# The adaLN modulation computed a channel chunk at a time on TensorE, ahead of the first four blocks' projections

## The chip, the cores and the metric

One core of one Trainium2 chip runs the whole layer in one launch. The metric is the device time of that launch in microseconds (us). The profile names the engines PE (TensorE; PEld is its weight load), DVE (VectorE), ACT (ScalarE), POOL (GpSimd) and SP (SyncE, which here only issues DMAs).

## The reference, cut to what matters

```python
mod = jax.nn.silu(c) @ w_ada + b_ada                 # c (1,1024), w_ada (1024,3072)
shift, scale, gate = jnp.split(mod, 3, axis=-1)
h = rms_norm(x, norm_w) * (1.0 + scale) + shift      # x (2048,1024)
z = h @ w_in                                         # w_in (1024,10240)
a, b, g_conv, q, k, v, g_attn, m_conv, m_attn = jnp.split(z, SPLIT_POINTS, axis=-1)
q = rope(rms_norm(q, q_norm_w), positions)           # 12 heads of 128; k likewise
k = rope(rms_norm(k, k_norm_w), positions)
...  # dilated window attention, convolution branch, gates, two output projections
return x + gate * out
```

The change concerns what comes ahead of the first product with `w_in`: `mod` for shift and scale, the normalized and modulated `h` of the first tokens, and the sines and cosines of `rope`.

## The kernel before, in words

Tokens are cut into 16 blocks of 128 (`NB`), channels into 8 chunks of 128 (`KC`). `h` is kept transposed in SBUF for the whole kernel, as a rounded part `hi` and the rest `lo`; every weight chunk likewise as `wh` and `wl`. A projection of one block sums 24 matmuls, three (`wh·hi`, `wl·hi`, `wh·lo`) for each channel chunk.

The kernel goes through 12 attention units (one head each; q, k and v, 384 columns), then the gates, the convolution branch and the output. Unit 0 is special: while it is projected, `h` is still being made. The steps of that stage are:

- `load_x(j)` loads 128 tokens and returns four steps: two ACT squares (L199) whose sums go to POOL (an addition, L202, then `rsqrt_cols`, L106 and L107), and two ACT scalings (L207). They are "normalizing x of block j". Six `x` tiles exist.
- `h_turn`/`h_part(j, kk)` turn two blocks and two channel chunks with PE transposes (L217), apply scale and shift on DVE (L238), round on ACT (L241) and subtract on DVE (L242). `h_first` does that for blocks 0 and 1 from four groups of transposes made early.
- `load_w` loads a chunk of weights (`raw`, three tiles), copies it on ACT (L281, `wh`) and subtracts (L284, `wl`; for unit 0 on POOL).
- `project_step(u, j)` runs the 24 matmuls (`z_tokens`, L305) with hooks between them, then "the rope" of the block: ACT squares and copies v (L322, L329), POOL raises to −1/2, DVE makes q and k and rotates them (L333 to L343), and SP stores the result (L656). In unit 0, block j's hooks at the 12th and 20th matmul turn blocks two ahead; hooks normalize x of block j + 4, loaded two blocks before.

Ahead of all this, modulation: `w_ada`'s first 2048 columns come as 16 DMAs of 512 KB (rows of 4 KB, ten tiles), and 64 matmuls with the one column `sc` as the stationary operand and 512 columns moving (L163) give rows of `mod`; ACT copies them, 16 small transposes make columns of them (L171), and DVE adds the bias. The rotary tables (`tab`) are made for all 16 blocks at once by 16 DVE operations of 1024 columns and two ACT sines.

The order on PE is the program's own (`manual_schedule`). On the other engines a scheduler chooses the order by its own estimates of times, except for instructions given to `keep_in_program_order`, which keep their order among each other. Each engine and SP's queue then run strictly in that order. A DMA also waits for the one that used its semaphore before it; eight are used in turn, so at most eight DMAs are under way.

Of the kernel before, what the change touches and what calls it, by code (L numbers as in the profile page):

```python
# [18 lines left out]
P = 128  # L19
# [35 lines left out]
def tile_hybrid_block(  # L55
# [55 lines left out]

    tab = tabs.tile([P, NB, 2, 64], F32, tag="tab", name="tab0")
    with pool("start", side="right") as st:
        nat = st.tile([4 * KC, P], F32, name="nat")
        cols = st.tile([P, 4 * KC], F32, name="cols")
        nc.sync.dma_start(nat[:KC, :], c.rearrange("b (k p) -> (b k) p", p=P))
        nc.sync.dma_start(nat[KC : 3 * KC, :], b_ada[: 2 * D].rearrange("(k p) -> k p", p=P))
        nc.sync.dma_start(nat[3 * KC :, :], norm_w.rearrange("(k p) -> k p", p=P))
        nc.sync.dma_start(wqk[:, 0, :], q_norm_w[None, :].to_broadcast([P, P]))
        nc.sync.dma_start(wqk[:, 1, :], k_norm_w[None, :].to_broadcast([P, P]))  # L120
        pos_i = st.tile([P, NB], I32, name="pos_i")
        nc.sync.dma_start(pos_i, positions.rearrange("b (j p) -> p (b j)", p=P))
        freq = st.tile([P, 64], F32, name="freq")
        nc.sync.dma_start(freq, inv_freq[None, :].to_broadcast([P, 64]))

        pt = bank("t", "pt_c")
        nc.tensor.transpose(pt[:, : 4 * KC], nat, ident[: 4 * KC, : 4 * KC])
        nc.vector.tensor_copy(cols, pt[:, : 4 * KC])
        th = st.tile([P, KC], F32, name="th_c")
        nc.scalar.activation(th, cols[:, :KC], AF.Tanh, scale=0.5)  # L130
        nc.vector.scalar_tensor_tensor(sc, th, 1.0, cols[:, :KC], op0=ALU.add, op1=ALU.mult)
        nc.vector.tensor_scalar(sc, sc, 0.5, None, op0=ALU.mult)

        pos_f = st.tile([P, NB], F32, name="pos_f")
        nc.vector.tensor_copy(pos_f, pos_i)
        a = tab[:, :, 0, :]
        n = tab[:, :, 1, :]
        nc.vector.tensor_tensor(a, pos_f[:, :, None].to_broadcast([P, NB, 64]),
                                freq[:, None, :].to_broadcast([P, NB, 64]), op=ALU.mult)

        na = st.tile([P, NB, 64], F32, name="na")
        nc.vector.tensor_scalar(n, a, 1.0 / (2 * math.pi), MAGIC, op0=ALU.mult, op1=ALU.add)
        nc.vector.tensor_scalar(n, n, -MAGIC, None, op0=ALU.add)
        nc.vector.tensor_scalar(na, n, MAGIC * 2048, None, op0=ALU.add)
        nc.vector.tensor_scalar(na, na, -MAGIC * 2048, None, op0=ALU.add)
        nc.vector.tensor_sub(n, n, na)
        for part in TWO_PI:
            for t in (na, n):
                nc.vector.scalar_tensor_tensor(a, t, -part, a, op0=ALU.mult, op1=ALU.add)
        nc.vector.tensor_scalar(a, a, -PI_LO, PI_LO, op0=ALU.max, op1=ALU.min)  # L150
        nc.scalar.activation(n, a, AF.Sin)
        nc.scalar.activation(a, a, AF.Sin, scale=0.5)
        tc.keep_in_program_order(nc.scalar.activation(th[:, :1], th[:, :1], AF.Exp))
        nc.vector.tensor_tensor(a, a, a, op=ALU.mult)
        nc.vector.tensor_scalar(a, a, -2.0, 1.0, op0=ALU.mult, op1=ALU.add)

        acc = [bank("z", "ada0"), bank("z", "ada1"), bank("s", "ada2"), bank("s", "ada3")]
        for k in range(KC):
            for half in range(2):
                wa = st.tile([P, D], F32, tag="wa", name=f"wada{k}_{half}", bufs=10)  # L160
                last_ada = nc.sync.dma_start(wa, w_ada[P * k : P * k + P, D * half : D * half + D])
                for i in range(2):
                    nc.tensor.matmul(acc[2 * half + i][:1, :], sc[:, k : k + 1], wa[:, 512 * i : 512 * i + 512],  # L163
                                     start=(k == 0), stop=(k == KC - 1))
        row = st.tile([1, 2 * D], F32, name="row")

        for i in range(4):
            nc.scalar.activation(row[:, 512 * i : 512 * i + 512], acc[i][:1, :], AF.Copy)
        pa = bank("z", "pt_ada")
        for k in range(2 * KC):  # L170
            nc.tensor.transpose(pa[:, k : k + 1], row[:, P * k : P * k + P], ident[:1, :1])  # L171
        nc.vector.tensor_add(mod, pa[:, : 2 * KC], cols[:, KC : 3 * KC])
        nc.vector.scalar_tensor_tensor(mod[:, KC:], mod[:, KC:], 1.0, cols[:, 3 * KC :], op0=ALU.add, op1=ALU.mult)

# [9 lines left out]
    xp = xpool_c.__enter__()  # L184
    hx = {}

    def load_x(j):

        xt = xp.tile([P, D], F32, tag="x", name=f"x{j}")
        i0 = nc.sync.dma_start(xt, x2[P * j : P * j + P, :])  # L190
        if j >= 4:
            tc.keep_in_program_order(i0)
# [51 lines left out]
    with tc.high_priority():  # L244
        for j in range(4):
            for f in load_x(j):
                f()
        turned = [h_turn(0, kk, "ttoo"[kk]) for kk in range(4)]


    spare = {}
# [865 lines left out]
```

## Time and profile before

| | us |
|---|---|
| three runs | 2533.59, 2529.49, 2529.74 |
| median | 2529.74 |
| the profiled execution | 2532.06 |
| its span (first to last instruction) | 2530.3 |
| PE busy in the span | 2495.4 |
| DVE, ACT, POOL busy | 1663.2, 756.8, 250.1 |

The profiled execution lies 2.3 us above the median of the runs; 1.8 us of it lie outside the span. PE is busy for 99% of the span, so what the kernel loses is found in the few places where PE is not. A "busy" PE can still be slow: matmuls are pipelined, and the clock that it is granted changes.

### The profile page before, as it was taken

To read this page: it belongs to the slowest core of one execution; us is meant where nothing else is said; L and a number is where in the kernel's file an instruction comes from. 1 tells how busy PE (TensorE), PEld (TensorE's weight loads), DVE (VectorE), ACT (ScalarE), POOL (GpSimd) and SP (SyncE) were. 2 spreads that over 40 slices of the span, in tenths; PEclk is the share of its full clock that TensorE was granted. 3 is DMA by queue.
4 is the path that set the end of the run, shared out by engine and by line. 5 is a ranking of instruction groups with operands and counts; after the bars stand their busy time and mean duration, and the time that the engine had idled before them with its cause. 6 is when DMAs were issued, how large, how long until landed. Compare 5 with 4: busy or idle time off the path is not lost.

```text
span 2530.3 us, 38239 instructions
## 1 busy us (share of the span) xinstructions
PE 2495.4 (99%) x13377; PEld 2222.5 (88%) x13377; DVE 1663.2 (66%) x3522; ACT 756.8 (30%) x2366; POOL 250.1 (10%) x503
## 2 busy tenths in 40 slices
PE   7999999999999999999999999999999999999999
PEld 3989999999999999999888888888888878888887
DVE  5855655555555555566799999879697718774333
ACT  5733343344334434444111111111111114331010
POOL 3421111111111111122000000000000000000000
PEclk9999999999999999999999999999999999999999
DMA  6333533344321111144112122121212249867343
GB/s 228 116 106 113 160 111 97 100 118 122 108 75 55 56 36 40 52 130 149 41 47 70 64 80 83 39 70 60 63 65 68 99 147 328 296 211 230 124 134 111
DMA packets 262653, 278.51 MB, mean 110 GB/s; under 512 B 25464, under 2 KB 195736, under 8 KB 262462
## 3 DMA queue, kind: packets, MB, share of 16 engines
q1 hardware_dynamic: 262462, 276.07, 34.3%
q8 instruction: 106, 1.74, 0.3%
q14 instruction: 85, 0.70, 0.1%
HBM read 175.12 MB, written 100.86 MB: 109 GB/s over the span
## 4 chain that ended last, share of the span: by engine, by line
PE 95%; DMA 2%; ACT 1%; DVE 1%; POOL 1%; issue 0%; SPq 0%; POOLq 0%; DVEq 0%; ACTq 0%
PE pz L305 30%; PE pg L755 20%; PE yc L897 7%; PE out L897 7%; PE pb L755 7%; PE pa L755 7%; PE ya L897 3%; PE pzg L305 3%; PE ps L377 3%; PE po L396 3%; PE ptq L367 2%; PE ptp L388 1%; PE ada L163 1%; DMA fraw<-in_w_attn_out_dram 1%; DMA raw_u<-in_w_in_dram 0%
## 5 line engine op out<-in xcount | busy, mean ns | idle before, releaser
L784 DVE SCALAR_TENSOR_TENSOR ca<-up,chan,ca 128x1024 f32<-128x1024 f32 x480 | 593.2, 1280 | 3.7
L305 PE MATMUL pz<-wh_u,hT_lo 128*128 128x384 f32 x1536 | 536.2, 349 | 1.3 <-POOL hT_lo L230 0.7
L305 PE MATMUL pz<-wh_u,hT_hi 128*128 128x384 f32 x1536 | 516.9, 337 | 5.3 <-ACT wh_u L281 2.6
L305 PE MATMUL pz<-wl_u,hT_hi 128*128 128x384 f32 x1536 | 517.7, 337 | 0.6 <-DVE wl_u L284 0.4
L333 DVE SCALAR_TENSOR_TENSOR qk<-pz,st,wqk 128x128 f32<-128x128 f32 x384 | 116.9, 346 | 332.2 <-POOL st L107 332.1
L755 PE MATMUL pg<-hT_hi,wh_gm 128*128 128x512 f32 x768 | 298.7, 389 | 0.3 <-DVE gt L815 0.3
L755 PE MATMUL pg<-hT_lo,wh_gm 128*128 128x512 f32 x768 | 298.6, 389 | 0.0
L755 PE MATMUL pg<-hT_hi,wl_gm 128*128 128x512 f32 x768 | 297.9, 389 | 0.0
L305 PEld LDWEIGHTS pz<-wh_u,hT_hi 128*128 128x128 f32 x1536 | 289.7, 189 | 8.7 <-ACT wh_u L281 3.5
L305 PEld LDWEIGHTS pz<-wh_u,hT_lo 128*128 128x128 f32 x1536 | 289.2, 188 | 3.5 <-POOL hT_lo L230 1.3
L305 PEld LDWEIGHTS pz<-wl_u,hT_hi 128*128 128x128 f32 x1536 | 288.8, 188 | 1.8 <-DVE wl_u L284 1.4
L369 ACT ACTIVATE qkT<-ptq 128x256 f32<-128x256 f32 x192 | 74.0, 385 | 419.2 <-PE ptq L367 418.6
L813 ACT ACTIVATE gt<-pg 128x512 f32<-128x512 f32 x96 | 57.1, 597 | 422.2 <-PE pg L755 422.2
L755 PEld LDWEIGHTS pg<-hT_hi,wh_gm 128*128 128x128 f32 x768 | 144.1, 188 | 30.7 <-DVE gt L815 0.7
L755 PEld LDWEIGHTS pg<-hT_hi,wl_gm 128*128 128x128 f32 x768 | 144.2, 188 | 30.0
L755 PEld LDWEIGHTS pg<-hT_lo,wh_gm 128*128 128x128 f32 x768 | 144.1, 188 | 29.7
L107 POOL TENSOR_TENSOR st<-st,mhalf 128x2 f32<-128x2 f32 x192 | 136.7, 712 | 16.0
L322 ACT ACTIVATE sq<-pz 128x128 bf16<-128x128 f32 x384 | 106.2, 277 | 93.2 <-PE pz L305 86.4
L106 POOL TENSOR_SCALAR st<-st 128x2 f32<-128x2 f32 x192 | 45.7, 238 | 811.8 <-ACT sq L322 811.8
L382 ACT ACTIVATE sm<-sm,osb 128x128 f32<-128x128 f32 (+1 forms) x192 | 88.8, 462 | 64.4 <-DVE osb L380 61.3
L755 PE MATMUL pb<-hT_hi,wh_ab 128*128 128x512 f32 x256 | 99.7, 389 | 0.0
L755 PE MATMUL pa<-hT_hi,wh_ab 128*128 128x512 f32 x256 | 99.6, 389 | 0.0
(332 smaller groups left out, 4639.0 us busy)
## 6 DMA issues: line engine op xcount, KB each, us to landing
qkv_d<-qkv SPq DMA_DIRECT2D x128, 192.0 KB, 2.2
raw_u<-in_w_in_dram SPq DMA_DIRECT2D x96, 192.0 KB, 3.1
lqk<-qkv_d SPq DMA_DIRECT2D x128, 128.0 KB, 2.2
acc_d<-osb SPq DMA_DIRECT2D x192, 65.0 KB, 1.6
at<-acc_d SPq DMA_DIRECT2D x64, 195.0 KB, 3.3
x<-in_x_dram SPq DMA_DIRECT2D x16, 512.0 KB
wada<-in_w_ada_dram SPq DMA_DIRECT2D x16, 512.0 KB, 7.1
lv<-qkv_d SPq DMA_DIRECT2D x128, 64.0 KB, 1.8
```

What stands on the lines that cost most here:

```text
L107: nc.gpsimd.tensor_tensor(dst, scratch[:, :n], mhalf[:, :n], op=ALU.pow)
L305: nc.tensor.matmul(pz[:, :width], a[:, k, P * j : P * j + P], w[:, :width], start=(m == 0), stop=(m == 23))
L322: nc.scalar.activation(sq, pz[:, P * i : P * i + P], AF.Square, scale=1.0 / math.sqrt(P), accum_out=st[:, i : i + 1])
L333: nc.vector.scalar_tensor_tensor(qk[:, 2 * i : 2 * i + 2].rearrange("p a b -> p (a b)"), pz[:, P * i : P * i + P], st[:, 2 + i : 3 + i], w ...
L369: nc.scalar.activation(qkT.rearrange("p a b -> p (a b)"), pt[:, :256], AF.Copy)
L377: nc.tensor.matmul(ps[:, P * i : P * i + P], box["q"][:, 0, :], kt[:, 1, :], start=True, stop=True)
L382: nc.scalar.activation(sm[:, :w], sm[:, :w], AF.Exp, scale=-1.0, bias=o[:, P : P + 1], accum_out=o[:, P + 1 : P + 2])
L396: nc.tensor.matmul(po[:, :P], box["pT"][:, P * i : P * i + P], vt, start=(i == 0), stop=(i == nk - 1))
L755: nc.tensor.matmul(pz, w[k][:, P * col : P * col + P], a[:, k, 512 * t : 512 * t + 512], start=(m == 0), stop=(m == 23))
L784: nc.vector.scalar_tensor_tensor(accs[c], up[:, t0 + i : t0 + i + 1024], chan[:, cb, i : i + 1], accs[c], op0=ALU.mult, op1=ALU.add)
L813: nc.scalar.activation(th, pz, AF.Tanh, scale=0.5)
L897: nc.tensor.matmul(pz, w, xx, start=(m == 0), stop=(m == len(terms) - 1))
```

## The change

The function for the first four blocks is written anew, behind the start of PE's manual order:

- `ada_part(c0)` makes shift and scale of one channel chunk: for each of the two halves, eight matmuls with a 128x128 piece of `w_ada` stationary and the one column `sc` moving. The result is a column in PSUM at once; DVE adds the bias to both (two pinned operations). `ada_load` brings the pieces, 32 DMAs of 256 KB in rows of 512 bytes, into eight tiles, which hold two chunks.
- `x_turn(k)` turns chunk k of four blocks; `h_make` applies scale and shift for 512 columns at once (ACT, DVE, DVE).
- `project_part(k)` adds chunk k to the four blocks' projections, which are kept open in four PSUM banks (two of tag `z`, two of `s`).
- The loop interleaves them: modulation of chunk k + 3 and loads of chunk k + 5, at h of chunk k and projection of chunk k − 1. Loads of weight chunks stand one chunk ahead.
- The tables are made in two halves of 8 blocks (512 columns), three operations at a time between those steps. ACT's two sines come in two pairs.
- The x loads of blocks 0 to 5 are issued by ACT instead of SP, and x of blocks 0 to 5 is normalized inside this part, in pinned order. Blocks 6 and 7 are loaded behind it, then blocks 4 and 5 are turned (`h_part(4, ·)`), then come the four ropes (`project_end`) and the loads of blocks 8 and 9.
- The main loop of unit 0 begins at block 4. Blocks 4 and 5 sum in a bank of tag `o`. `lo_last` (block 0's products with `lo` last), the early Exp table load, the row copies and the 16 small transposes are gone. Six tile kinds of the attention steps move to a pool `att`, opened at block 14 in the space that the start leaves.

```diff
-        acc = [bank("z", "ada0"), bank("z", "ada1"), bank("s", "ada2"), bank("s", "ada3")]
-        for k in range(KC):
-            for half in range(2):
-                wa = st.tile([P, D], F32, tag="wa", name=f"wada{k}_{half}", bufs=10)
-                last_ada = nc.sync.dma_start(wa, w_ada[P * k : P * k + P, D * half : D * half + D])
-                for i in range(2):
-                    nc.tensor.matmul(acc[2 * half + i][:1, :], sc[:, k : k + 1], wa[:, 512 * i : 512 * i + 512],
-                                     start=(k == 0), stop=(k == KC - 1))
...
+    def ada_load(c0):
+        for half in range(2):
+            c1 = D * half + P * c0
+            view = w_ada[:, c1 : c1 + P].rearrange("(k p) c -> p k c", p=P)
+            for q in range(2):
+                wa = was[c0, half, q] = st.tile([P, 4, P], F32, tag="wa", name=f"wada{c0}_{half}_{q}", bufs=8)
+                keep(nc.sync.dma_start(wa, view[:, 4 * q : 4 * q + 4]))
+    def ada_part(c0):
+        pa = bank("o", f"pa{c0}")
+        for half in range(2):
+            for k in range(KC):
+                nc.tensor.matmul(pa[:, half : half + 1], was[c0, half, k // 4][:, k % 4], sc[:, k : k + 1],
+                                 start=(k == 0), stop=(k == KC - 1))
...
+    def h_make(k, pt):
+        scale, shift = mod[:, KC + k : KC + k + 1], mod[:, k : k + 1]
+        hs = hi[:, k, : P * FIRST]
+        keep(nc.scalar.activation(hs, pt, AF.Identity, scale=scale, bias=shift))
+        hf = xp.tile([P, 512], F32, tag="hf", name=f"hf0_{k}", bufs=2)
+        keep(nc.vector.tensor_scalar(hf, pt, scale, shift, op0=ALU.mult, op1=ALU.add))
+        keep(nc.vector.tensor_tensor(lo[:, k, : P * FIRST], hf, hs.bitcast(F32), op=ALU.subtract))
...
+        normed = {j: load_x(j, nc.scalar) for j in range(FIRST)}
+        ada_load(0)
+        ada_load(1)
...
+        for j in range(FIRST):
+            for f in normed.pop(j):
+                keep(f())
...
+        angle_steps(12)
+        for i in range(3):
+            ada_part(i)
+            ada_load(i + 2)
+            angle_steps(3)
+            if i == 1:
+                rests.append(loads[0]())
+        for k in range(KC):
+            h_make(k, x_turn(k))
+            rests.pop(0)()
+            if k + 1 < KC:
+                rests.append(loads[k + 1]())
+            angle_steps(3)
+            if k + 3 < KC:
+                ada_part(k + 3)
+                if k + 5 < KC:
+                    ada_load(k + 5)
+            if k >= 1:
+                project_part(k - 1)
+            if k == 1:
+                normed = {j: load_x(j, nc.scalar) for j in range(FIRST, FIRST + 2)}
+                norms = [f for j in range(FIRST, FIRST + 2) for f in normed.pop(j)]
+            if k >= 4:
+                keep(norms.pop(0)())
+                keep(norms.pop(0)())
+        project_part(KC - 1)
+    normed.update((j, load_x(j)) for j in range(FIRST + 2, FIRST + 4))
+    angle_steps(100)
...
+    for kk in range(4):
+        h_part(FIRST, kk)
+    for j in range(FIRST):
+        nc.sync.dma_start(qkv_d[0][P * j : P * j + P], project_end(0, j, tab, pzs[j]))
...
+    normed = {j: load_x(j) for j in range(FIRST + 4, FIRST + 6)}
...
-            for j in range(NB):
+            for j in range(0 if u else FIRST, NB):
```

What this does to the order is seen at three places. The first is PE at the end of modulation. In the names, `ada` and `pa` are sums of the modulation, `wada` pieces of `w_ada`, `pz_0` the projection of block 0, and `pt_x` transposes of x. Before, this stands there:

```order
L163 MATMUL ada_154<-wada_1_216,sc 1x512
L163 MATMUL ada_155<-wada_1_216,sc 1x512
L171 MATMUL pt_ada<-ident,row 128x1 x16
L305 MATMUL pz_0_417<-wh_u_0_327,hT_hi 128x384
L305 MATMUL pz_0_417<-wl_u_0_328,hT_hi 128x384
```

And now, at the first product of the projections:

```order
L480 MATMUL pt_x_1_364<-ident,x_150 128x128
L469 MATMUL pa_382<-sc,wada_0_0_308 128x1 x4
L469 MATMUL pa_382<-sc,wada_0_1_310 128x1 x4
L469 MATMUL pa_382<-sc,wada_1_0_312 128x1 x4
L469 MATMUL pa_382<-sc,wada_1_1_314 128x1 x4
L495 MATMUL pz_0_205<-wh_u_0_286,hT_hi 128x384
L495 MATMUL pz_0_205<-wl_u_0_287,hT_hi 128x384
```

The projections no longer wait for the last sum of the modulation: that of the fifth chunk (`pa_382`) stands ahead of them, three more stand between them.

The second place is ACT around the normalizing of x of block 3 (`x_289` before, `x_150` now). Before:

```order
L207 ACTIVATE x_278<-x_278,xst_281 128x512 x2
L199 ACTIVATE xn_291,xst_292<-x_289 128x512
L207 ACTIVATE x_289<-x_289,xst_292 128x512 x2
L281 ACTIVATE wh_u_6_363<-raw_u_6_361 128x384
L281 ACTIVATE wh_u_7_369<-raw_u_7_367 128x384
L151 ACT_TABLE_LOAD
L151 ACTIVATE tab_107<-tab_107 128x16x64
```

Now:

```order
L135 ACTIVATE xn_152,xst_153<-x_150 128x512 x2
L143 ACTIVATE x_150<-x_150,xst_153 128x512 x2
L519 ACT_TABLE_LOAD
L519 ACTIVATE tab_107<-tab_107 128x8x64
L520 ACTIVATE tab_107<-tab_107 128x8x64
L200 ACTIVATE wh_u_0_286<-raw_u_0_284 128x384
L486 ACTIVATE hT_hi<-pt_x_0_319,mod 128x512
```

The weight copies, eight of them ahead of the sines before, now come behind the sines, each with the chunk that it serves; the first sines stand between the last scaling and the first chunk of `hi`.

The third place is ACT where x of block 8 is normalized (`x_559` before, `x_819` now; `sq_4`, `sq_5` are the ropes of blocks 4 and 5). Before:

```order
L199 ACTIVATE xn_561,xst_562<-x_559 128x512 x2
L241 ACTIVATE hT_hi<-hf_0_732 128x2x256
L207 ACTIVATE x_559<-x_559,xst_562 128x512 x2
L322 ACTIVATE sq_4_761,st_4_762<-pz_4_709 128x128
L241 ACTIVATE hT_hi<-hf_1_751 128x2x256
L322 ACTIVATE sq_4_761,st_4_762<-pz_4_709 128x128
L329 ACTIVATE qkv_4_765<-pz_4_709 128x128
```

Now:

```order
L242 ACTIVATE sq_5_956,st_5_957<-pz_5_904 128x128 x2
L164 ACTIVATE hT_hi<-hf_2_927 128x2x256
L164 ACTIVATE hT_hi<-hf_3_946 128x2x256
L249 ACTIVATE qkv_5_960<-pz_5_904 128x128
L135 ACTIVATE xn_821,xst_822<-x_819 128x512 x2
L135 ACTIVATE xn_825,xst_826<-x_823 128x512 x2
L143 ACTIVATE x_819<-x_819,xst_822 128x512 x2
```

Block 8's x was normalized before the rope of block 4; it now comes behind that of block 5. Behind unit 0 the order on PE is the same as before.

More of the change, by code (lines that the diff above doesn't have):

```diff
@@ L491, in tile_hybrid_block @@
     main, beside = Flow(), Flow()
+    att = {}
     HOOK, HOOK2 = 14, 5
@@ L520, in tile_hybrid_block @@
     pe_order.__enter__()
+    FIRST = 4
+    st_c = pool("start", side="right")
+    st = st_c.__enter__()
+    keep = tc.keep_in_program_order
+    nat = st.tile([4 * KC, P], F32, name="nat")
+    cols = st.tile([P, 4 * KC], F32, name="cols")
+    pos_i = st.tile([P, NB], I32, name="pos_i")
+    pos_f = st.tile([P, NB], F32, name="pos_f")
+    freq = st.tile([P, 64], F32, name="freq")
+    th0 = st.tile([P, KC], F32, name="th_c")
+    was = {}
+    def ada_load(c0):
[5 more added lines that the diff above has]
+                keep(nc.sync.dma_start(wa, view[:, 4 * q : 4 * q + 4]))
@@ new lines, in sines, with cosines @@
+    def sines(j0, count):
+        a, n = tab[:, j0 : j0 + count, 0, :], tab[:, j0 : j0 + count, 1, :]
+        keep(nc.scalar.activation(n, a, AF.Sin))
+        yield nc.scalar.activation(a, a, AF.Sin, scale=0.5)
+    def cosines(j0, count):
+        a = tab[:, j0 : j0 + count, 0, :]
+        yield nc.vector.tensor_tensor(a, a, a, op=ALU.mult)
+        yield nc.vector.tensor_scalar(a, a, -2.0, 1.0, op0=ALU.mult, op1=ALU.add)
+    later = angles(8, 8)
+    turning = itertools.chain(angles(0, 8), sines(0, 8), itertools.islice(later, 5), cosines(0, 8), later,
+                              sines(8, 8), cosines(8, 8))
```

163 lines of the change are left out of this document (75 added, 88 removed).

## The prediction, made before the changed kernel ran

> **What bounds the kernel now.** I read the table of stages first (busy us of PE, PEld, DVE, ACT, POOL with counts, granted clock, DMA share, GB/s), because the page calls PE busy for 99% and hides where it is not.
>
> ```profile
> 0.00:24.10 24.10, 9.48 (x25) 4.05 (x26) 9.03 (x12) 14.59 (x32) 14.29 (x29) 1.00 0.84 273
> 24.10:50.50 26.40, 25.35 (x73) 5.69 (x71) 12.27 (x12) 8.90 (x14) 2.85 (x2) 1.00 0.79 297
> 50.50:73.40 22.90, 21.67 (x128) 19.77 (x129) 20.53 (x48) 18.57 (x52) 10.77 (x22) 1.00 0.15 45
> 73.40:120.60 47.20, 44.62 (x274) 42.34 (x273) 39.64 (x102) 36.22 (x107) 20.18 (x40) 1.00 0.40 130
> 120.60:141.60 21.00, 18.49 (x108) 17.21 (x106) 15.77 (x42) 8.15 (x30) 5.96 (x8) 1.00 0.29 91
> 141.60:2000.00 1858.40, 1853.52 (x10488) 1708.21 (x10489) 1298.01 (x2908) 548.27 (x1949) 191.02 (x394) 1.00 0.26 82
> 2000.00:2530.30 530.30, 522.29 (x2289) 425.23 (x2287) 267.91 (x403) 122.14 (x187) 5.06 (x8) 0.99 0.60 195
> ```
>
> From 141.6 us on PE idles 4.9 and 8.0 us in 2389, and its order there does not change. So what the start gains or loses until unit 1 begins in earnest reaches the end. That point and the modulation, in PE's timeline and in the chain of waits (start, duration, what):
>
> ```profile
> 50.51 0.44 PE L305 MATMUL pz<-wh_u,hT_hi 128*128 128x384 f32 x1 [1.06 <-ACT hT_hi L223]
> 141.65 0.44 PE L305 MATMUL pz<-wh_u,hT_hi 128*128 128x384 f32 x1 [2.42 <-ACT wh_u L281]
> ...
> 19.02 29.34 PE ada L163 x64
> 147.12 15.53 PE pz L305 x88
> ```
>
> Modulation holds PE for 29.34 us; the first projection starts at 50.51. After it DVE is fuller than ACT, but it waits for what PE and ACT bring; ACT is 18.57 + 36.22 = 54.8 us busy in the 70.1 us from 50.5 to 120.6, where the last block's x is scaled, and its waits are the ones that last. ACT's groups from 60 to 120.6 us (busy, mean ns | idle before, releaser), and that last scaling:
>
> ```profile
> L207 ACT ACTIVATE x<-x,xst 128x512 f32<-128x512 f32 x22 | 14.8, 715 | 11.0 <-POOL xst L107 11.0
> L199 ACT ACTIVATE xn<-x 128x512 bf16<-128x512 f32 x22 | 13.9, 630 | 0.2
> L241 ACT ACTIVATE hT_hi<-hf 128x512 fp32r<-128x512 f32 x21 | 13.1, 624 | 0.1
> L322 ACT ACTIVATE sq<-pz 128x128 bf16<-128x128 f32 x22 | 5.8, 263 | 1.7 <-PE pz L305 1.6
> L329 ACT ACTIVATE qkv<-pz 128x128 f32<-128x128 f32 x11 | 3.0, 271 | 0.0
> ...
> 119.95 0.71 ACT L207 ACTIVATE x<-x,xst 128x512 f32<-128x512 f32 x1
> ```
>
> One x costs ACT 2 x 0.715 + 2 x 0.63 and the reads of two sums, about 3 us, and ACT waits 11.0 us in all for POOL's power. So three things carry the start: modulation until 50.5, ACT's normalizing until 120.6, then 21 us to unit 1, whose work and order stay. I therefore follow one event, the last scaling, 120.6 now.
>
> **First part: x of blocks 0 to 3.** Prices: the first square; POOL's chain alone (from 11.38) and beside DVE's table work (the 2.54); table load, sine, weight copy; four transposes cold and warm; two matmuls with a full fp32 stationary operand.
>
> ```profile
> 4.51 0.63 ACT L199 ACTIVATE xn<-x 128x512 bf16<-128x512 f32 x1 [2.51 <-DMA x<-in_x_dram]
> 5.18 0.52 ACT L281 ACTIVATE wh_u<-raw_u 128x384 fp32r<-128x384 f32 x1
> 22.78 1.33 ACT L207 ACTIVATE x<-x,xst 128x512 f32<-128x512 f32 x2 [2.54 <-POOL xst L107]
> 31.08 1.28 ACT L151 ACT_TABLE_LOAD   x1
> 34.39 1.06 ACT L151 ACTIVATE tab<-tab 128x1024 f32<-128x1024 f32 x1 [2.02 <-DVE tab L150]
> ...
> 11.38 0.19 POOL L202 TENSOR_TENSOR xst<-xst 128x1 f32<-128x1 f32 x1 [0.97 <-ACT xn L199]
> 11.97 0.58 POOL L107 TENSOR_TENSOR xst<-xst,mhalf 128x1 f32<-128x1 f32 x1
> ...
> 15.07 2.82 PE L217 MATMUL pt_x<-ident,x 128*128 128x128 f32 x12 [1.05 <-ACT x L207]
> 53.08 0.60 PE L217 MATMUL pt_x<-ident,x 128*128 128x128 f32 x4
> 53.44 0.42 PE L305 MATMUL pz<-wl_u,hT_hi 128*128 128x384 f32 x1
> 703.10 0.39 PE L377 MATMUL ps<-qkT 128*128 128x128 f32 x2
> 703.32 0.38 PE L367 MATMUL ptq<-ident,lqk 128*128 128x128 f32 x2
> ```
>
> The x loads now stand on ACT's queue behind positions and frequencies, and ACT issues four of them before its table load and the tanh; so its first square starts about 1.5 us later than now, at 6. Per x it does squares (1.5), waits for POOL, scales (1.33), and the pinned order lets nothing in between. POOL's wait is 1.2 alone and 2.5 while DVE makes tables, which it does for the first three: 6 + 4 x 2.83 + 3 x 2.4 + 1.3 = 25.8, against 24.1 now. Bounds 22 (always 1.2) and 28. SP's nat loads move to the head of its queue and cost nothing. POOL's weight subtractions move behind the four chains; they are needed only after 30.
>
> Until the first projection: table load 1.28, two sines of half width 1.1, weight copy 0.5, `hi` 0.6, then on DVE the scaling of 512 columns and the subtraction, about 0.9 + 0.65 (rows below), together with hand-overs 5.5: 31.3. PE needs in that time two groups of transposes and two chunk sums. **A chunk sum is the operation that this trace does not show**: 16 matmuls, 128x128 fp32 stationary, one column moving. Its nearest row is the score matmul, the same operand with 128 columns, two in 703.32 − 703.10 = 0.22: 0.11 each, 1.8 a chunk. The bounds are the warm transpose, 0.36 for four, 1.4 a chunk, and the cold one, 2.82 for twelve, 3.8 a chunk. I take 1.8. Three chunk sums run before x is ready, which costs nothing unless DMA is late; the sums and transposes from 25.8 to 31.3 fit even half cold.
>
> **Second part: the eight chunks.** From 31.3 PE has 96 products at 15.53/88 = 0.176 (16.9), sums of the last three chunks (5.3), six groups of transposes (2.2): 24.4 us, so 55.7. DVE has 3 to 4 us per chunk (three table steps, two small additions, scaling, subtraction), no more than PE's 4.1, but on POOL's port: hidden, or up to 0.5 a chunk if not. The loads are the other limit:
>
> ```profile
> wada<-in_w_ada_dram SPq DMA_DIRECT2D x16, 512.0 KB, 7.1
> 20.00:40.00 20.00, 20.00 (x45) 3.74 (x43) 15.93 (x14) 7.51 (x11) 5.11 (x5) 1.00 1.04 395
> 130.50:142.00 11.50, 9.08 (x51) 8.36 (x49) 6.53 (x18) 3.15 (x11) 3.03 (x4) 1.00 0.38 116
> DMA to landing us min/median/max: 3.9/6.2/9.0
> ```
>
> With 4 KB rows all engines full carry 395 GB/s; with the 512-byte pieces of weights, 116/0.38 = 305. Until the last chunk there are to load 8.4 MB of `w_ada`, 3.1 of x, 1.0 of weights: 12.5 MB in 41 us, from 2.5 on, so the last chunk is there at about 44, when PE could use it at 43 to 44. I add 1.3 for this: the four projections end at T = 57 (54 to 65). The Trainium skill ("DMA: Bandwidth & Descriptors", Specifications) has 512 bytes as the size from which a transfer runs at line rate. By that the last chunk lands near 34, the 1.3 falls away and the sum comes out 1.3 lower; the two rates above speak against it.
>
> **Third part: from T to the last scaling.** ACT's work is what it does now from 50.5 to 120.6 without the first `hi` of two blocks (3.1 of it lie there), x of blocks 4 and 5 (6.2, done before T in ACT's gaps), and the turn of blocks 2 and 3 (4 x 0.62): 54.8 − 11.8 = 43. Its waits for POOL are 1.0 for each of ten x: 10. New are waits that now hide behind an even flow: at T four ropes and the turn of blocks 4 and 5 fall due at once. DVE's prices:
>
> ```profile
> 129.01 1.00 DVE L238 TENSOR_SCALAR hf<-pt_x,mod 128x256 f32<-128x256 f32 x2
> 130.32 1.29 DVE L242 TENSOR_TENSOR hT_lo<-hf,hT_hi 128x512 fp32r<-128x512 f32 x2
> 132.52 0.61 DVE L333 SCALAR_TENSOR_TENSOR qk<-pz,st,wqk 128x128 f32<-128x128 f32 x2 [0.90 <-POOL st L107]
> 134.17 0.28 DVE L343 TENSOR_TENSOR qkv<-qkv,t 128x128 f32<-128x128 f32 x1
> ```
>
> A rope is 134.45 − 132.52 = 1.9. Until the last `lo` of blocks 4 and 5 DVE does four pairs of scalings (4), four subtractions (2.6) and most of three ropes (5.5): T + 13 with its start. Block 4 ends at T + 14, block 5 (24 products and eight transposes, 4.9) at T + 19. ACT has meanwhile two x, four ropes at 0.8 and some eight roundings, 14.5: it waits 4.5, because the order puts x of block 8 behind block 5's rope (SP sends its load only behind the store of block 3, so an earlier place would not help much). About 3 more it waits for DVE's scalings of blocks 6 and 7, which stand behind two ropes. Together T + 43 + 10 + 7.5 = T + 60.5 = 117.5. PE meanwhile idles some 7 us at block 4 and 6 at block 6, where its transposes need x of blocks 8 and 9: most of the 29 us that modulation no longer holds comes back there.
>
> **The sum.** 120.6 − 117.5 = 3.1 us earlier, carried to the end: 2532.06 − 3.1 = 2529.0 for an execution like the profiled one, which lies 2.3 above the median, so 2526.7 for the median. Small edits go along at nothing, each with its cover: SP's 32 loads for 16 (half a microsecond each, under loads of 4 us a chunk), the moved q/k norm loads (needed only at the first rope), the second pair of sines (ACT has gaps at chunk 4), the Exp table load that now falls in unit 1 (PE runs projections), the pool `att` (opened when the start is long done). If a cover is missing, each costs about 1 us. Behind 2000 us the scheduler orders ACT, DVE and SP a little differently; I allow 2 us either way.
>
> **Rivals.** A measurement of this kernel can tell about 0.2%, 5 us, from no change.
>
> *The gain holds (faster).* If POOL's chain takes 1.2 throughout and DMA keeps ahead, T is 53; if half of the 7.5 us of new waits is hidden, the last scaling falls at 53 + 57 = 110: 10.6 earlier, 2519. For it speaks that PE has 29 us less to do there and that POOL's long waits were in part behind weight subtractions which are gone from that stretch; against it ACT's 43 + 10.
>
> *The ring of eight tiles starves PE (slower).* Before, ten tiles of 512 KB were under way and a load landed 7.1 us after its issue. Now two chunks, 2.1 MB, are, and a freed tile is refilled only after PE's sum. At 7.1 us that is 295 GB/s, about what I used; at the 9.0 that a 512-byte load has taken, 233, and 12.5 MB take 54 us. The last chunk then lands at 56, T is about 67, and the kernel ends 7 later than before: 2537. The point from which it decides is landing after some 8.3 us. Against it: the median of those loads is 6.2.
>
> *The clock stays low (slower).*
>
> ```profile
> 143.05 0.52 PE L305 MATMUL pz<-wh_u,hT_hi 128*128 128x384 f32 x1
> 143.37 0.52 PE L305 MATMUL pz<-wl_u,hT_hi 128*128 128x384 f32 x1
> 142.00:147.50 5.50, 4.70 (x15) 3.47 (x15) 4.02 (x11) 2.39 (x9) 1.03 (x2) 0.69 0.42 125
> ```
>
> After 2.4 us of idling a product takes 0.32 and the granted clock is 0.69. If one-column sums and waits keep it there through the eight chunks, 96 products cost 14 us more: T is 71, the end 11 us later than before, 2541. From six in ten of the products cold on (8 us late) it is slower by over 5. Against it: with 21.67 of 22.9 us busy the clock was 1.00. The Trainium skill ("TensorE: Matmul & The Clock Gate", Part 1) gives full clock after about 3.4 us of sustained work and half after an idle window as long; the first rows of modulation agree in kind, and no row shows one-column matmuls.
>
> **How the numbers follow.** Within 5 us of before (3 faster): 0.42. The gain holds: 0.33. Ring or clock: 0.16 and 0.07, and 0.02 for slower otherwise, 0.25. The likeliest case's own range is 2525 to 2532. The range that leaves out no more than 2 in 10 reaches into both: 2517 to 2538.
>
> **What would show it.** Modulation gone as one block from PE's chain; chunk sums at 1.4 to 1.8 us; x of block 3 scaled near 26; four projections done near 57; PE idle at block 4 and in block 6; last scaling near 117; the third weight wait of unit 1 near 138. I am wrong if ACT's waits after T are far from 17, if a chunk sum takes over 2.5, or if SP waits for landings rather than PE's sums.

## The result: slower by 33.7 us

| | us |
|---|---|
| before, median of 4 runs | 2529.61 (2529.18 to 2533.59) |
| changed kernel, median of 4 runs | 2563.27 (2562.35 to 2565.18) |
| ratio | 1.013, 95% interval 1.0113 to 1.0148 |
| its profiled execution, and span | 2565.18, 2563.3 |

The prediction said 2527 and a range of 2517 to 2538. The stages of the changed kernel, cut at the events that the prediction named (the same columns as its first fence):

```profile
0.00:33.20 33.20, 20.95 (x97) 20.76 (x98) 11.16 (x25) 15.34 (x30) 8.62 (x24) 1.00 0.76 215
33.20:48.35 15.15, 15.15 (x74) 15.15 (x74) 9.96 (x17) 2.60 (x4) 2.17 (x2) 1.00 0.66 193
48.35:87.56 39.21, 39.08 (x217) 38.08 (x218) 17.02 (x28) 14.46 (x30) 6.91 (x11) 0.83 0.41 121
87.56:150.50 62.94, 48.94 (x283) 44.86 (x282) 48.24 (x124) 44.18 (x131) 22.41 (x52) 0.92 0.33 109
150.50:172.00 21.50, 19.07 (x113) 17.99 (x111) 15.56 (x43) 7.52 (x28) 7.64 (x8) 1.00 0.29 88
```

The first projection starts at 48.35 (predicted 31.3), the four projections are done at T = 87.56 (57), the last scaling of x ends at 150.5 (117.5), and ACT's copy that ends the third weight wait of unit 1 starts at 172.0, against 141.1 before. The loss is complete at T: 30.6 us. From 14 to 87 us PE has no idle time to speak of, so nothing that PE waits for explains it. PE's own timeline does (start, duration, what):

```profile
14.41 18.93 PE L469 MATMUL pa<-sc,wada 128*128 128x1 f32 x88 [2.75 <-DMA wada<-in_w_ada_dram]
33.20 1.09 PE L480 MATMUL pt_x<-ident,x 128*128 128x128 f32 x4
34.09 6.83 PE L469 MATMUL pa<-sc,wada 128*128 128x1 f32 x32
40.77 1.09 PE L480 MATMUL pt_x<-ident,x 128*128 128x128 f32 x4
41.66 6.83 PE L469 MATMUL pa<-sc,wada 128*128 128x1 f32 x32
48.35 0.67 PE L495 MATMUL pz<-wh_u,hT_hi 128*128 128x384 f32 x1
48.81 0.52 PE L495 MATMUL pz<-wl_u,hT_hi 128*128 128x384 f32 x1
...
52.99 3.91 PE L469 MATMUL pa<-sc,wada 128*128 128x1 f32 x32
56.76 0.67 PE L495 MATMUL pz<-wh_u,hT_hi 128*128 128x384 f32 x1
57.23 0.52 PE L495 MATMUL pz<-wl_u,hT_hi 128*128 128x384 f32 x1
...
59.71 0.34 PE L495 MATMUL pz<-wh_u,hT_hi 128*128 128x384 f32 x1
59.88 0.34 PE L495 MATMUL pz<-wl_u,hT_hi 128*128 128x384 f32 x1
...
60.67 4.68 PE L469 MATMUL pa<-sc,wada 128*128 128x1 f32 x32
```

Two things stand in it. A chunk sum has 32 records for its 16 matmuls: each float32 matmul runs as two passes. And a pass costs 0.215 us (18.93 / 88) as long as PE does little else, 0.122 (3.91 / 32) in the sum behind the first run of products, and 0.119 in the one behind the third. The products that follow a sum start at 0.32 apart (57.23 to 57.55). They come to 0.175 only 2.9 us later (59.71 to 59.88); in the first and third run not before the transposes behind them, 4.4 and 4.6 us after the run's start. "Cold" and "warm" stand for these two paces below.

That the pace is the clock is seen from 56 us on, where the granted clock (the third figure from the end) falls with it:

```profile
52.00:56.00 4.00, 4.00 (x34) 3.90 (x33) 1.96 (x2) 1.30 (x2) 1.00 (x1) 1.00 0.33 80
56.00:60.00 4.00, 4.00 (x17) 4.00 (x17) 2.57 (x6) 0.00 (x0) 0.00 (x0) 0.57 0.89 246
...
64.00:68.00 4.00, 4.00 (x16) 4.00 (x16) 1.84 (x5) 0.00 (x0) 0.00 (x0) 0.50 0.17 49
```

The first of these stretches holds the warm sum, the other two hold products at 0.32. Up to 48 us the same column reads 1.00, though passes take 0.215; that the clock is low there too is inferred from the time of a pass.

The two passes were to be read before, and so was the cold price of a pass: the prediction's twelve cold transposes took 2.82 / 12 = 0.235 each. That passes of one column keep PE cold was not. These are groups of the kernel before, by line:

```profile
L377 PE MATMUL ps<-qkT 128*128 128x128 f32 x384 | 74.0, 275 | 0.0
L388 PE MATMUL ptp<-ident,sm 128*128 128x128 f32 x300 | 63.8, 273 | 0.0
L377 PE MATMUL ps<-qkT,qkT 128*128 128x128 f32 x216 | 41.8, 275 | 0.0
```

The code issues one score matmul (L377) for each transpose of the probabilities (L388). There are 300 of these, and 384 + 216 = 600 records of scores. So the row that the prediction divided by two ("x2", 0.22 us) was one matmul in two passes, not two matmuls.

### The profile page after: what moved, and what is told of

Its sections match the earlier page's. It is cut to its first block, busy times and chain, and to the rows that moved or that the text cites. A ratio compares the mean times of both kernels' runs of the same rounds, so it can differ in the third digit from the quotient of the medians.

```text
span 2563.3 us, 38627 instructions
## 1 busy us (share of the span) xinstructions
PE 2521.9 (98%) x13553; PEld 2273.3 (89%) x13553; DVE 1668.9 (65%) x3545; ACT 755.7 (29%) x2359; POOL 243.6 (10%) x499
## 4 chain that ended last, share of the span: by engine, by line
PE 95%; DMA 1%; ACT 1%; DVE 1%; POOL 1%; issue 0%; SPq 0%; POOLq 0%; ACTq 0%
PE pz L222 29%; PE pg L824 20%; PE yc L966 7%; PE out L966 7%; PE pa L824 7%; PE pb L824 7%; PE ya L966 3%; PE pzg L222 3%; PE ps L297 3%; PE po L316 3%; PE pa L469 2%; PE ptq L287 2%; PE ptp L308 1%; PE pz L495 1%; DMA wada<-in_w_ada_dram 0%; DMA raw_u<-in_w_in_dram 0%
## 5 line engine op out<-in xcount | busy, mean ns | idle before, releaser
L222 PE MATMUL pz<-wh_u,hT_lo 128*128 128x384 f32 x1504 | 527.1, 350 | 1.3 <-DVE hT_lo L165 1.1
L222 PE MATMUL pz<-wh_u,hT_hi 128*128 128x384 f32 x1504 | 507.6, 337 | 3.8 <-ACT wh_u L200 2.8
L222 PE MATMUL pz<-wl_u,hT_hi 128*128 128x384 f32 x1504 | 508.2, 338 | 0.0
L824 PE MATMUL pb<-hT_lo,wh_ab 128*128 128x512 f32 x256 | 99.6, 389 | 0.0
```

The lines of the kernel that those rows point to most:

```text
L222: nc.tensor.matmul(pz[:, :width], a[:, k, P * j : P * j + P], w[:, :width], start=(m == 0), stop=(m == 23))
L824: nc.tensor.matmul(pz, w[k][:, P * col : P * col + P], a[:, k, 512 * t : 512 * t + 512], start=(m == 0), stop=(m == 23))
```

## Experiments

Theory A: the two passes of the sums' matmuls, and a clock that does not stay up under passes of one column, take the time on PE. Theory B: only the number of passes counts, not the clock. Theory C: the loads through a ring of eight tiles bound the start. A second pair concerns the stretch behind T. Of all kernels T (the start of block 4's transposes) and the span of the profiled execution tell the same story:

| kernel | T | span | span − T | ratio to before (95%) |
|---|---|---|---|---|
| the change | 87.56 | 2563.3 | 2475.7 | 1.0130 (1.0113 to 1.0148) |
| 128 equal columns | 65.21 | 2537.2 | 2472.0 | 1.0028 (1.0017 to 1.0038) |
| 64 equal columns | 79.86 | 2554.3 | 2474.4 | one run |
| 32 equal columns | 86.02 | 2557.4 | 2471.4 | one run |
| 4 of 16 matmuls | 61.54 | 2535.5 | 2474.0 | 1.0017 (1.0008 to 1.0027) |
| no reload | 90.72 | 2563.9 | 2473.2 | 1.0130 (1.0115 to 1.0145) |
| row sums | 73.38 | 2548.5 | 2475.1 | 1.0070 (1.0055 to 1.0085) |
| interleaved | 98.95 | 2571.2 | 2472.3 | 1.0160 (1.0145 to 1.0176) |
| x early | 87.87 | 2554.1 | 2466.2 | 1.0091 (1.0078 to 1.0105) |
| 128 columns, x early | 64.98 | 2531.8 | 2466.8 | 1.0002 (0.9993 to 1.0010) |
| one pass, x early | 97.25 | 2563.4 | 2466.2 | 1.0127 (1.0114 to 1.0141) |
| one pass ahead, x early | 67.87 | 2533.6 | 2465.7 | 1.0024 (1.0014 to 1.0034) |

T runs from 61 to 99, and the rest stays within 4.3 us without and 1.1 us with the second edit: what happens before T reaches the end one to one. The medians below come from several sessions: the kernel before had 2529.61 beside the change and 2531.5 to 2532.4 beside the other kernels, so ratios and spans compare better than medians do.

### 128 equal columns: the clock alone

```diff
-                nc.tensor.matmul(pa[:, half : half + 1], was[c0, half, k // 4][:, k % 4], sc[:, k : k + 1],
+                nc.tensor.matmul(pa[:, P * half : P * half + P], was[c0, half, k // 4][:, k % 4],
+                                 sc[:, k : k + 1].to_broadcast([P, P]), start=(k == 0), stop=(k == KC - 1))
```

> The chunk sums keep their 16 matmuls with the full 128x128 piece of the weights stationary, but move 128 equal columns (the column sc repeated) instead of one. Nothing else changes on any engine. Theory A (the sums' two passes per matmul, and a clock that does not stay up under one-column matmuls, bound the start): the passes cost the same as with one column when the clock is up, about 0.11 us, and the clock now stays up. The three sums ahead of the first x take about 12 us instead of 20, the first product comes near 34 instead of 48, products cost 0.176 instead of 0.32, and the four projections are done near 64 instead of 87.5; the kernel ends near 2540. Theory B (only the number of passes counts, the clock has no part in it): 128 columns are no cheaper than one, the projections are done at 87 or later, 2563 to 2575. Theory C (loads of the pieces through eight tiles bound the start): no change, 2563.

Measured: median 2539.26, T 65.21. In PE's timeline:

```profile
13.42 12.70 PE L469 MATMUL pa<-sc,wada 128*128 128x128 f32 x88 [1.79 <-DMA wada<-in_w_ada_dram]
25.96 0.94 PE L480 MATMUL pt_x<-ident,x 128*128 128x128 f32 x4
26.74 3.74 PE L469 MATMUL pa<-sc,wada 128*128 128x128 f32 x32
...
34.25 0.42 PE L495 MATMUL pz<-wh_u,hT_hi 128*128 128x384 f32 x1
34.51 0.34 PE L495 MATMUL pz<-wl_u,hT_hi 128*128 128x384 f32 x1
```

128 times the arithmetic, and T is 22 us earlier, as theory A forecast (34, 64 and 2540). About the first 32 passes are still cold; every sum from the fourth chunk on costs 3.74, products are at 0.17 from the first, and the order on the other engines is the same to the last instruction. Theory B falls. Of the 30.6 us that T was late, 22.4 go with the clock. The other 8.2 are, by the rows, mostly the second pass: the first product comes 3.0 later than predicted, behind two sums of 3.5 from start to start, and the three sums of the loop take 10.5 instead of 5.3.

### A quarter of the sums

The products k = 0 and 4 stay, the others are left out; the loads stay.

```diff
             for k in range(KC):
+                if k % 4:
+                    continue
                 nc.tensor.matmul(pa[:, half : half + 1], was[c0, half, k // 4][:, k % 4], sc[:, k : k + 1],
-                                 start=(k == 0), stop=(k == KC - 1))
+                                 start=(k == 0), stop=(k == 4))
```

> Each chunk sum issues 4 of its 16 matmuls (k = 0 and 4 of each half); the other 12 products are left out of shift and scale. All loads and waits stay. Theory A: a chunk sum costs 8 passes, 1.7 us cold and 0.9 warm, instead of 32 at 3.6 to 6.8; x of block 3 (27.5 us) then decides when the first product starts, near 33, and the four projections are done near 56 to 60, the kernel near 2533. Theory C: the loads are the same, so the projections end where they did, 87, and the kernel at 2563.

Measured: 2537.28, T 61.54, all loads as before. A sum took 1.71 us for eight cold passes and 0.95 for eight warm ones, as expected. T lies 1.5 past the expected range: PE now waits 7.2 us in all for landings (two of 0.46 to 0.47 in the last sum), and some products are cold. The scheduler also put ACT, DVE and SP in a somewhat different order here, which the run does not take apart.

### No reload: the ring

```diff
         for half in range(2):
+            if c0 > 1:
+                for q in range(2):
+                    was[c0, half, q] = was[c0 - 2, half, q]
+                continue
```

> Only the first two chunks of w_ada are loaded; the sums of chunks 2 to 7 read those eight tiles again, so 24 of the 32 loads are left out and nothing waits for the ring. Theory A: the four projections are still done near 87 and the kernel ends at 2563, within 4. Theory C: with the loads gone the projections are done near 57 to 64, the kernel near 2535.

The sums of chunks 2 to 7 read the first eight tiles again. Measured: 2565.73, T 90.72. With 24 of 32 loads gone nothing is gained, so theory C falls for the change as it stands. In the changed kernel itself SP waits for the sums, and a piece lands in 4.2 us (minimum, median, maximum):

```profile
SPq L463 <- PE pa L469: 27.0, 21, 4.5
...
DMA to landing us min/median/max: 3.0/4.2/4.5
```

### Row sums: the operands exchanged

```diff
-                nc.tensor.matmul(pa[:, half : half + 1], was[c0, half, k // 4][:, k % 4], sc[:, k : k + 1],
-                                 start=(k == 0), stop=(k == KC - 1))
+                    nc.tensor.matmul(pa[:1, P * half : P * half + P], sc[:, k : k + 1], was[c0, half, k // 4][:, k % 4],
+                                     start=(k == 0), stop=(k == KC - 1))
```

> The roles of the sums' operands are exchanged: the one column sc is stationary and the 128 columns of a piece of w_ada move, as the kernel before did with 512. A chunk sum is again 16 matmuls, now giving a row of 256; DVE copies it and two small transposes make the columns, one chunk later. By the row of the kernel before (0.458 us for 512 columns) a matmul costs 0.115 and a chunk sum 1.8, the price that the prediction had taken. Theory A: the three sums ahead of x hide behind it, the first product starts near 33.5, the clock stays up, the four projections are done near 59, and the kernel ends near 2535: with its own price of a chunk sum the prediction's second part holds. Theory C: no change, 2563. If the sums cost this and the products still take 0.32, the clock falls for another reason, the projections are done near 66 and the kernel ends near 2542.

Measured: 2550.97, T 73.38: better than the change, far from 2535. My price was wrong again:

```profile
13.95 8.99 PE L472 MATMUL pa<-wada,sc 128*1 128x128 f32 x56 [2.28 <-DMA wada<-in_w_ada_dram]
...
27.79 3.65 PE L472 MATMUL pa<-wada,sc 128*1 128x128 f32 x32
...
35.35 5.32 PE L472 MATMUL pa<-wada,sc 128*1 128x128 f32 x32 [3.11 <-DVE mod L486]
```

A sum is again 32 passes, of 0.114 each: a matmul with 128 columns costs 0.23, half of the 0.458 that one with 512 costs, not a quarter. The clock stays up, as theory A has it, except in the sum behind the wait of 3.11. Most of the 8 us to the kernel with 128 columns are the wait of 3.11 for DVE's additions (the columns are turned one chunk later), the cold sum behind it (5.32 for 3.65), and two small transposes per chunk.

### Interleaved: does a finer mixture keep the clock?

In each `ada_part` of chunks 4 to 7 a product is issued ahead of three of four matmuls of the sum, in place of `project_part` behind it:

```diff
+        between = project_list(kp) if kp is not None else []
         for half in range(2):
             for k in range(KC):
+                if between and (KC * half + k) % 4 != 3:
+                    between.pop(0)()
```

> Order on PE alone: the sums of the fifth to eighth chunk, one column moving as in the change, are no longer one block of 16 matmuls but alternate with the 12 products of the projections that follow them. Theory A with the clock (a block of one-column matmuls of 4 us counts as idle for the clock, and the products behind it start at half speed): sprinkled among products the sums leave the clock up; of the 48 products of that stretch none costs 0.32, the sums cost 3.6; the four projections are done near 78 instead of 87.5, and the kernel ends near 2554. If the clock goes by the share of columns moved over some microseconds, alternating does not help: products stay at 0.30 to 0.34, and the kernel ends at 2561 to 2565.

Measured: 2573.13, T 98.95, 11.4 later than in the change; the span is 7.9 longer. The products do not pull the sums up, the sums pull the products down:

```profile
52.75 0.67 PE L496 MATMUL pz<-wh_u,hT_hi 128*128 128x384 f32 x1
53.22 0.42 PE L472 MATMUL pa<-sc,wada 128*128 128x1 f32 x2
53.50 0.67 PE L496 MATMUL pz<-wl_u,hT_hi 128*128 128x384 f32 x1
53.97 0.42 PE L472 MATMUL pa<-sc,wada 128*128 128x1 f32 x2
```

Through 46 us (40.6 to 86.3) a product and the matmul behind it take 0.75 us, 0.47 and 0.28, and two passes start 0.21 apart; PE shows no idle time. In blocks the products at least come up at the end of a run of twelve or just behind it. So the first reading on record falls, that only a block of one-column matmuls counts as idle. The second, that the share of time in which columns move counts, had the cold products right; the end at 2561 to 2565 it had too early.

### 32 and 64 columns: how wide is wide enough

The edit is that of 128 columns with another number.

> As the kernel with 128 equal columns, with 32: how wide must the moving side be for the clock to come up? If the clock goes by the share of time in which columns stream, 32 columns fill about a quarter of what 128 do and the sums stay cold as with one: passes at 0.21, the four projections done near 87, 2560. If any stream wider than one column does, it is as with 128: passes at 0.117 and the kernel near 2539.

> The same with 64 equal columns. By the share of time the answer lies between: the clock comes up later or not at all, the kernel between 2539 and 2560. If 64 are enough, passes cost 0.117 or a little less and the kernel ends near 2539.

Measured, one run each: 2559.28 (T 86.02) and 2556.18 (T 79.86). The first sums, with 32 and then with 64 columns:

```profile
14.53 18.98 PE L469 MATMUL pa<-sc,wada 128*128 128x32 f32 x88 [2.73 <-DMA wada<-in_w_ada_dram]
...
60.68 3.66 PE L469 MATMUL pa<-sc,wada 128*128 128x32 f32 x32
...
66.79 4.21 PE L469 MATMUL pa<-sc,wada 128*128 128x32 f32 x32
```

```profile
13.52 19.03 PE L469 MATMUL pa<-sc,wada 128*128 128x64 f32 x88 [1.97 <-DMA wada<-in_w_ada_dram]
...
51.55 3.68 PE L469 MATMUL pa<-sc,wada 128*128 128x64 f32 x32
55.04 0.42 PE L495 MATMUL pz<-wh_u,hT_hi 128*128 128x384 f32 x1
```

Neither width brings the clock up from cold: passes stay at 0.215 through 19 us. With 64 columns, once products have warmed PE, it stays warm through every later sum; with 32 it falls in two of three (one of them the 4.21), with one it falls each time.

How much of a pass do the columns fill? This is an estimate from two paces. The float32 matmuls with 512 columns of the kernel before (one record each) start 0.429 us apart once warm, 0.84 ns a column; the float32r products start 0.173 apart with 384, 0.45 ns a column. Warm passes start 0.112 apart, so 128 float32 columns fill 96% of one, 64 fill 48%, 32 fill 24%, and one fills 1%; cold, pass and column take about twice as long, and the shares stay. In the alternation above, products fill at most 0.32 of 0.75 us, 43%. So of these streams the one that fills nearly all of the time brought the clock up, and those that fill half or less did not. Half held it through sums of 3.5 us, a quarter held it once in three. That the share decides is argued from these kernels; none tests it alone.

### x of blocks 8 and 9 ahead of the stores

```diff
+    early = {j: load_x(j) for j in range(FIRST + 4, FIRST + 6)}
     for j in range(FIRST):
         nc.sync.dma_start(qkv_d[0][P * j : P * j + P], project_end(0, j, tab, pzs[j]))
...
-    normed = {j: load_x(j) for j in range(FIRST + 4, FIRST + 6)}
+    normed = early
```

> Only the loads of x of blocks 8 and 9 are moved: on SP's queue they now stand ahead of the stores of the first four ropes instead of behind them. In the changed kernel the load was issued at 106.7, behind stores that wait for the ropes, and PE waited 9.8 us in block 6 for these x. Theory P (the place in SP's queue makes that wait): x of block 8 is there near 92, the wait falls below 2 us, the last scaling comes about 7 us earlier, and the kernel ends near 2556. Theory Q (ACT's own work and its waits carry that stretch; the x is late anyway): the wait moves to another place on ACT or DVE and the kernel ends at 2561 to 2563.

Measured: 2555.83, 7.4 less than the change by the medians, 9.9 by the two ratios; the span is 9.2 us shorter. SP's queue in the change and then with this edit:

```profile
93.12 13.52 SPq L590 DMA_DIRECT2D qkv_d<-qkv  x4
106.73 1.35 SPq L128 DMA_DIRECT2D x<-in_x_dram  x3
```

```profile
84.95 0.91 SPq L128 DMA_DIRECT2D x<-in_x_dram  x2
...
94.26 12.62 SPq L591 DMA_DIRECT2D qkv_d<-qkv  x4
```

Theory P holds: the load is issued 22 us earlier. PE's wait for these x fell from 9.8 to 4.2, not below 2; behind what is left stand ACT's waits for POOL ahead of the two scalings (3.1 and 0.4). More came back than the 5.6 of this wait. The order of ACT and DVE changed with the edit too, at about 70 places each; what that is worth was not separated.

### Both edits

> The two edits together: 128 equal columns in the sums, and the loads of x of blocks 8 and 9 ahead of the stores. By theory P the wait of 8.7 us in block 6 goes, and the kernel ends 7 below the one with 128 columns alone, that is within 2 us of the kernel before (ratio 0.998 to 1.002). By theory Q it stays at 1.003.

Measured: 2532.67, ratio 1.0002 (0.9993 to 1.0010): as expected by theory P, and no better than the kernel before. From 100 to 140 us PE is then busy for 39.64 of 40 us, so the time that five sums of 3.74 take between the products of the start is not given back by any wait behind them.

### One pass: float32r sums

To take the second pass away, pieces and `sc` are rounded to float32r (`war`, `scr`), at first directly ahead of each sum:

```diff
+                if c0 < 3:
+                    keep(nc.vector.tensor_copy(war[q], was[c0, half, q]))
+                else:
+                    keep(nc.scalar.activation(war[q], was[c0, half, q], AF.Copy))
...
+                nc.tensor.matmul(pa[:, P * half : P * half + P], war[k // 4][:, k % 4],
+                                 scr[:, k : k + 1].to_broadcast([P, P]), start=(k == 0), stop=(k == KC - 1))
```

> As the kernel with both edits, but the pieces of w_ada and the column sc are rounded to float32r first (by DVE for the first three chunks, by ACT for the other five; six raw tiles and two rounded ones in the space of eight), so that a matmul of the sum needs one pass instead of two. Theory A: a chunk sum of 16 passes costs 1.8 us, the price that the prediction had taken; the four projections are done near 57 and the kernel ends some 7 us below the one with both edits, ratio to before 0.997. If the rounding on ACT (five times 4 x 0.62 us) or the smaller ring becomes the limit, the projections are done no earlier than 64, and the ratio stays at 1.000.

Measured: 2564.80, T 97.25, 32 us above the kernel before where 7 below were expected. PE waited 35.2 us for the rounding (13.7 of it ahead of the first sum), and with such gaps 16 passes are as slow as 32 warm ones:

```profile
46.52 3.85 PE L483 MATMUL pa<-scr,war 128*128 128x128 f32 x16 [3.11 <-ACT war L480]
```

ACT and PE had become one chain: turn, `hi`, rounding, sum, next turn. The second form rounds one step ahead and loads the raw weights one chunk earlier:

> The kernel with both edits and one-pass sums again, with the two chains taken apart that held its first form: each chunk is rounded one step of the loop ahead of its sum (into four rounded tiles beside four raw ones; by DVE for four chunks, by ACT for the other four), and the raw weights are loaded one chunk ahead of the weight copy. Theory A: with nothing in between PE runs a chunk in 0.44 (turn) + 1.85 (16 passes) + 2.1 (12 products); the four projections are done near 57, and the kernel ends 7 to 9 us below the one with both edits, ratio to before 0.997. If four raw tiles of 256 KB are too few (1 MB in 4.2 us, 250 GB/s), PE waits for rounding behind landings, the projections are done near 64 and the ratio is 1.000.

Measured: 2537.52, T 67.87, ratio 1.0024; 27 us came back. Once warm, a sum costs 1.98. Before that it costs 3.7. In the first 30 us PE waits between sums; but from 29.93 on it has hardly a gap, and still two more sums and the first twelve products (at 0.32) are cold, until 42.9:

```profile
29.93 3.65 PE L498 MATMUL pa<-scr,war 128*128 128x128 f32 x16 [0.33 <-DVE war L481]
...
34.23 3.73 PE L498 MATMUL pa<-scr,war 128*128 128x128 f32 x16
...
53.45 1.98 PE L498 MATMUL pa<-scr,war 128*128 128x128 f32 x16
```

With 128 columns in two passes the clock came up after some 32 passes. By the estimate above, 128 float32r columns fill only half of a pass, so taking the second pass away would also take away what warmed PE. With four raw tiles, ACT also waits for landings:

```profile
ACT war L483 <- DMA wada<-in_w_ada_dram: 7.2, 10, 2.5
```

So the ring binds ACT here, as the rival in its expectation had it, but PE waited only 1.6 us for ACT's rounding. It waited 13.6 for DVE's, all of it before 30 us, and DVE 5.5 for landings. How the 10.9 us by which T is late divide between cold passes and landings was not tested. No kernel of this study beat the one before.

## Why the prediction was wrong

**The failed term is the price of a chunk sum, 1.8 us.** It measured 6.7 to 6.8 cold and 3.7 to 4.6 in the loop. The nearest row was well chosen, but misread: 0.22 is the price of one score matmul. Even the upper bound of 3.8 came from one pass (the cold transpose), while the sum has two. With 0.22 the sum had been 3.5 warm, and with the cold row doubled 7.5: the rows held the answer.

**The low clock was a rival with 7 in 100, and it happened.** Its condition, that one-column sums keep the clock down, is what the runs showed. Its price counted products alone and left the sums warm; the 128 columns took 22.4 us off T. Of the products themselves, the seven runs in the timeline add up to 24.3 us instead of 16.9. "Busy" PE was taken as evidence against it, and that was the error of reasoning: one-column passes fill the busy column and move next to nothing. The Trainium skill ("TensorE: Matmul & The Clock Gate", Part 1) ties the fall of the clock to an idle window of about 3.4 us. It gives full speed after about 3.4 us of sustained work, and the 2.9 to 4.6 us in which products came up again agree in kind; but PE had no idle time by its rows when the clock fell, 2.4 to 3.3 us into the sums, so the rule as it is worded does not cover this, and the measurement decides.

**T, term by term.** First product: 31.3 predicted, 48.35 measured. x was nearly in time (last scaling from 26.27 on for 1.33, 27.6 against 25.8), but PE ended its third sum only at 33.2, and two more of 6.8 with two turns followed. From there 25.7 predicted, 39.2 measured: three sums +6.6, products +7.4, turns +0.7, and the 1.3 for loads not needed.

**Behind T the total held, in part by luck.** Predicted were 43 us of ACT's work and 17.5 of waits to the last scaling, 60.5; measured 44.18 and 18.76, 62.9. The work was right. The waits were not the predicted ones (us in total, times, longest):

```profile
ACT qkv L249 <- DMA qkv_d<-qkv: 5.7, 3, 2.3
ACT hT_hi L164 <- DVE hf L161: 4.3, 6, 1.4
ACT x L143 <- POOL xst L108: 4.2, 5, 1.3
ACT xn L135 <- DMA x<-in_x_dram: 3.2, 1, 3.2
```

For POOL 10 were predicted and 4.2 came. The copies of v waited 5.7 for the ropes' stores, which the prediction does not have; that these two nearly cancel is luck. The other 7.5, for x of block 8 and for DVE, came as 3.2 and 4.3. PE's idle time there was predicted at 7 and 6, and is 62.94 − 48.94 = 14.0, but 9.8 of it lie in block 6, which has the predicted cause:

```profile
115.39 0.47 PE L153 MATMUL pt_x<-ident,x 128*128 128x128 f32 x1 [8.44 <-ACT x L143]
117.22 0.90 PE L153 MATMUL pt_x<-ident,x 128*128 128x128 f32 x3 [1.36 <-ACT x L143]
```

From the last scaling to the copy that ends the third weight wait of unit 1 it is 21.5 us against 20.4 before, and from there to the end of the span 2391.3 against 2389.2; where these last 2.1 us lie was not followed. Together the part behind T is some 5.6 us longer than predicted: with T at 57 this kernel would end near 2533 and not 2527, so that even sums of 1.8 us on a warm PE would have left it beside the kernel before.

**The other rivals.** The ring did not starve PE (the run without reloads). That the gain holds had little to stand on: PE needs 29.3 us for the sums in the form before and 8 x 3.74 = 29.9 in the best two-pass form here, and only three of the eight stand ahead of the first turn of x, where PE has nothing else to do. The prediction saw that the load of block 8's x stands behind the stores, and took it as a reason why an earlier place in ACT's order "would not help much"; it gave the load's own place no price. Moving the load was worth 7 to 10 us.

## What to carry to other kernels

Count a row's records against the matmuls that the code issues before dividing by them; a float32 matmul with 128 or fewer columns is two records here. A matmul that moves few columns cost as much here as one that moves 128, and it also cooled PE for the work behind it, so either widen it, or put it where PE has slack; to sprinkle it among good products cost 7.9 us more. A busy column of 100% says nothing of speed: look at the distance from one start to the next.

## What the runs showed of the hardware that was not expected

- A pass with a full 128x128 stationary operand costs 0.215 us cold with 1, 32, 64 or 128 columns moving, and 0.112 warm with any of them, from start to start (0.115 to 0.122 as the length of a row by its passes). The Trainium skill ("TensorE: Matmul & The Clock Gate", LDWEIGHTS (loading the stationary operand)) gives P / 1.2 ns for loading a stationary operand of P columns, by estimate 107 ns for 128; the warm passes agree, the cold ones take twice that.
- PE can be busy without a gap for 46 us at half speed (the interleaved kernel). In the changed kernel it came up 2.9 to 4.6 us after wide products began to run alone, and fell 2.4 to 3.3 us into a sum of one-column passes.
- The clock in the profile's rows does not show this: in the same 46 us it reads 1.00, as it does from 0 to 48 us in the changed kernel, where every pass is cold. It shows only later falls (0.83 from 48.35 to 87.56).
